# Norm weights turned by TensorE, the first two transfers mixed by chunks, the last left half in two pieces, and a new table of due times

## The chip, the cores and the metric

The kernel runs on one core of one Trainium2 chip. The metric is the device time of one execution, in microseconds (us). The kernel before takes 917.24 us, the median of three runs (917.19 to 917.48).

A core has TensorE (PE in the profile; its weight loads are PEld), VectorE (DVE), ScalarE (ACT), GpSimd (POOL) and SyncE (SP). Each works through its own list in order and waits on counts (semaphores) that the others raise. Transfers are issued by SP, ACT or POOL and carried out by 16 shared DMA engines.

## The reference, cut to what matters

One layer of a decoder trunk on x (512 positions x 1024) and a memory of 256 rows x 1024, all float32.

```python
h = rmsnorm(x, norm_mix_g);  proj = h @ w_in            # 9216 columns
y_a = (gb * conv3(gc * v)) @ w_a_out                    # short gated convolution
y_b = silu(layernorm(conv31(u * sigmoid(ug)))) @ w_b_out
memn = rmsnorm(mem, norm_mem_g);  k, vm = split(memn @ w_kv)
y_c = softmax(q k^T / 16) vm @ w_att_out                # 4 heads
x = x + (sum_i sigmoid(gate_i) * y_i) @ w_o
x = x + (silu(gt) * up) @ w_down                        # gt, up = split(conv3(rmsnorm(x) @ w_up))
return rmsnorm(x, norm_final_g)
```

## The kernel before, in words

Everything is on one core, with the features on the 128 partitions. A product is made of three matmuls: each operand is split into a rounded part (`whi`, `mh`, `zh`; a cast on ACT) and the rest (`wlo`, `ml`, `zl`; a subtraction on DVE), and hi x hi, lo x hi and hi x lo are added up in a PSUM bank (`product`). Weights come in units of 128 x 1024 (512 KB). SP fetches most of them; POOL adds sums of weight blocks by transfers of its own.

**The order of the work** is made when the program is built. PE's order is a list (`seq`), changed by MOVES. All other work is given as jobs, each with an engine, an estimated cost, what it needs and what it frees. `Jobs.run` then hands out the jobs: each job has a due time, counted back from the PE work that needs it, shifted by the table LATER, and AHEAD says how long before it the job may start. The result is one fixed list per engine.

**The start.** `jobs.first` lists the first transfers of SP: the first half of the memory (`mem`, turned by the host, 4 chunks of 128 features x 256 rows), then the first key unit of `w_kv` (`wf`), then value and key units. ACT issues one transfer of the norm weights (`pk`, 128 x 16: 8 columns of the memory's norm, 8 of the first norm of x). Meanwhile PE runs 11 products of a constant (L2101), which serve no result. ACT scales the 4 chunks by the norm weight (`mg0`, L950); then PE makes the first keys with 8 float32 products (L1142), 2 for each chunk, straight from `mg0` and the unit as it was fetched. After them come the values (L630 to L632), which need `mh`, `ml` (from `mg0`) and `whi`, `wlo` of the value unit in halves (L1087, L1091).

**The end of the up-projection.** The gated product `z` (L2069) is split into `zh`, `zl` and goes into the down-projection. In the same place DVE also splits weight units (`wlo`, L683) and combines PSUM banks (`uu`, L636), which gives a bank back to PE.

**The end.** Row tile 3 comes last. Its squares are summed, ACT takes the root (L2449), DVE the reciprocal (L2497). ACT scales the right half (L2455) and issues its store; DVE scales the left half with the norm weight (L2459, 128 x 512), and SP stores it.

## Time and profile before

| | |
|---|---|
| median of 3 runs | 917.24 us |
| profiled execution | 917.32 us |
| its span, first to last instruction | 915.5 us |
| PE busy | 906.7 us (99%) |
| DVE busy | 848.1 us (93%) |
| ACT busy | 685.3 us (75%) |
| PE's waits of over 0.15 us | 0.9, 1.0 and 0.5 us |
| DMA, mean over the span | 215 GB/s |

PE's matmuls overlap, and their ends are modelled: a PE that is busy all the time can still lose tenths of a microsecond between two matmuls. So the start of a matmul against the start of the one before is read as well. What lies ahead of PE's first product of use and behind its last one counts in full.

### The profile page before, as it was taken

The page shows a single profiled execution, that of the slowest core. Times are in us where ns is not written, and L with a number is a line of the kernel's source. Part 1 is how long each engine was busy: PE and PEld are TensorE (multiplying, and loading weights), DVE is VectorE, ACT ScalarE, POOL GpSimd, SP SyncE. Part 2 cuts the span into 40 slices and gives each one's busy share as a digit, 9 for nine tenths or more (in the row PEclk, how much of TensorE's full clock was granted, in tenths as well). Part 3 has the DMA queues.
Part 4 walks back from the last instruction along what each step waited for, and adds up shares of the span by engine and source line. Part 5 has one row for each costly group of instructions (what it writes and reads, how often), then busy time and mean ns, then how long its engine had stood idle before and what let it go on. Part 6 is the DMA issues. An engine that isn't in the chain of part 4 may idle for free.

```text
span 915.5 us, 17045 instructions
## 1 busy us (share of the span) xinstructions
PE 906.7 (99%) x6789; PEld 856.9 (94%) x6789; DVE 848.1 (93%) x965; ACT 685.3 (75%) x940; POOL 137.5 (15%) x164
## 2 busy tenths in 40 slices
PE   9999999999999999999999999999999999999997
PEld 8999999999989999999899997899999999988886
DVE  6996999999999998999898999898969899999987
ACT  7777979988987875979758973767757676865566
POOL 0111212000011111110101211121212021001400
PEclk9999999999999999999999999999999999999999
DMA  9998888644699878977868999999999677679972
GB/s 366 371 305 183 177 197 179 144 113 96 172 242 256 202 156 212 218 155 208 209 135 230 204 252 323 244 234 298 273 244 243 171 170 157 171 267 313 278 142 93
DMA packets 55377, 196.91 MB, mean 215 GB/s; under 512 B 6273, under 2 KB 6401, under 8 KB 55297
## 3 DMA queue, kind: packets, MB, share of 16 engines
q0 software_dynamic: 22608, 81.54, 49.3%
q1 hardware_dynamic: 32400, 114.02, 34.5%
q8 instruction: 53, 0.87, 0.4%
q10 hardware_dynamic: 288, 0.27, 0.1%
q14 instruction: 28, 0.22, 0.1%
HBM read 191.60 MB, written 4.19 MB: 214 GB/s over the span
## 4 chain that ended last, share of the span: by engine, by line
PE 95%; DVE 2%; ACT 1%; issue 1%; DMA 1%; SPq 0%; DVEq 0%; ACTq 0%
PE bank L862 63%; PE bank L632 6%; PE bank L630 6%; PE bank L631 6%; PE bank L1702 3%; PE bank L1700 3%; PE bank L1701 3%; PE bank L1153 2%; DVE wlo L683 1%; PE bank L1934 1%; DVE gtc L1656 1%; DMA wf<-in_w_kv 1%; PE bank L1142 0%; ACT whi L679 0%; PE bank L1989 0%
## 5 line engine op out<-in xcount | busy, mean ns | idle before, releaser
L679 ACT CAST whi<-wf 128x1024 fp32r<-128x1024 f32 (+1 forms) x199 | 207.1, 1044 | 88.8 <-PE bank L862 44.4
L683 DVE TENSOR_TENSOR wlo<-wf,whi 128x1024 fp32r<-128x1024 f32 (+1 forms) x193 | 232.1, 1211 | 16.1 <-ACT whi L679 15.8
L1468 ACT ACTIVATE tp<-u,pk 128x511 f32<-128x511 f32 (+22 forms) x184 | 119.0, 704 | 3.8 <-DVE acc L1475 3.2
L1475 DVE TENSOR_TENSOR acc<-acc,tp 128x1018 f32<-128x1018 f32 (+22 forms) x92 | 109.2, 1188 | 6.5 <-ACT tp L1468 4.7
L804 POOL DMA_DIRECT2D wf<-in_w_in x44 | 39.9, 937 | 204.4 <-DVE wlo L683 140.9
L862 PE MATMUL bank<-ft6h,whi 128*128 128x256 f32 x248 | 68.6, 277 | 0.5 <-ACT gt L889 0.5
L862 PE MATMUL bank<-fb10h,whi 128*128 128x256 f32 x248 | 68.7, 277 | 0.0
L862 PE MATMUL bank<-fb11h,whi 128*128 128x256 f32 x248 | 68.7, 277 | 0.0
L862 PE MATMUL bank<-ft7h,whi 128*128 128x256 f32 x248 | 68.6, 277 | 0.0
L862 PE MATMUL bank<-fb00l,whi 128*128 128x256 f32 x248 | 68.6, 276 | 0.0
L862 PE MATMUL bank<-ft7l,whi 128*128 128x256 f32 x248 | 68.5, 276 | 0.0
L862 PE MATMUL bank<-ft6l,whi 128*128 128x256 f32 x248 | 68.5, 276 | 0.0
L862 PE MATMUL bank<-ft5l,whi 128*128 128x256 f32 x248 | 68.5, 276 | 0.0
L862 PE MATMUL bank<-ft7h,wlo 128*128 128x256 f32 x248 | 68.5, 276 | 0.0
L862 PE MATMUL bank<-fb00h,whi 128*128 128x256 f32 x248 | 68.5, 276 | 0.0
L862 PE MATMUL bank<-ft5h,whi 128*128 128x256 f32 x248 | 68.5, 276 | 0.0
L862 PE MATMUL bank<-ft4h,whi 128*128 128x256 f32 x248 | 68.5, 276 | 0.0
L862 PE MATMUL bank<-ft6h,wlo 128*128 128x256 f32 x248 | 68.5, 276 | 0.0
L862 PE MATMUL bank<-ft4l,whi 128*128 128x256 f32 x248 | 68.5, 276 | 0.0
L862 PE MATMUL bank<-fb11l,whi 128*128 128x256 f32 x248 | 68.5, 276 | 0.0
L862 PE MATMUL bank<-fb10l,whi 128*128 128x256 f32 x248 | 68.5, 276 | 0.0
L862 PE MATMUL bank<-ft5h,wlo 128*128 128x256 f32 x248 | 68.5, 276 | 0.0
(414 smaller groups left out, 3165.3 us busy)
## 6 DMA issues: line engine op xcount, KB each, us to landing
wf<-in_w_in SPq DMA_DIRECT2D x52, 512.0 KB, 5.6
wf<-in_w_in POOLq DMA_DIRECT2D x44, 512.0 KB, 7.3
wf<-in_w_up SPq DMA_DIRECT2D x30, 512.0 KB, 7.8
wf<-in_w_up POOLq DMA_DIRECT2D x29, 512.0 KB, 8.1
wf<-in_w_down SPq DMA_DIRECT2D x15, 512.0 KB, 5.4
wf<-in_w_kv SPq DMA_DIRECT2D x8, 512.0 KB, 9.0
wf<-in_w_v SPq DMA_DIRECT2D x8, 512.0 KB, 7.9
wf<-in_w_att_out SPq DMA_DIRECT2D x8, 512.0 KB, 3.7
```

The lines of the kernel that those rows point to most:

```text
L630: nc.tensor.matmul(ps, s_hi, w_hi, start=start, stop=False, skip_group_check=again)
L631: nc.tensor.matmul(ps, s_hi, w_lo, start=False, stop=False, skip_group_check=again)
L632: nc.tensor.matmul(ps, s_lo, w_hi, start=False, stop=stop, skip_group_check=again)
L679: nc.scalar.copy(parts[0], src())
L683: nc.vector.tensor_tensor(lo, src(), hi.bitcast(F32), op=ALU.subtract)
L804: nc.gpsimd.dma_start(out=tiles[key], in_=block(w, col[c], k), accum_op=ALU.add)
L862: nc.tensor.matmul(to, w[:, k, at], col, start=first and n == 0, stop=k == 3 and n == 2, skip_group_check=again,)
L1468: nc.scalar.activation(two(("tp", p, s))[:, j, s:], two(("u", p))[:, j, : SEQ - s], AF.Copy, scale=weight(j),)
L1475: nc.vector.tensor_tensor(a, a, two(("tp", p, s))[:, :, s:], op=ALU.add)
L1700: nc.tensor.matmul(ps, w_hi[:, i, at], hi, start=first, stop=False)
L1701: nc.tensor.matmul(ps, w_hi[:, i, at], lo, start=False, stop=False)
L1702: nc.tensor.matmul(ps, w_lo[:, i, at], hi, start=False, stop=last)
```

## The change

**What is computed** stays the same. Five things are done in another way.

1. The host packs the first memory half and the first key unit into one array `first` of two parts: part e has chunks 2e and 2e+1 of both. SP fetches the two parts, 512 KB each, in place of the memory half and the unit.
2. The norm weights come as 16 rows of 128. PE turns them with a transposition between 6 and 4 products of the constant (10 in place of 11), and DVE copies the 16 columns out of the bank. `mg0` waits for that copy.
3. The 4 scaled chunks are made by ACT (0 and 2) and DVE (1 and 3) in place of ACT alone.
4. The last left half is scaled and stored in two pieces of 256 columns.
5. LATER, AHEAD, FRESH and MOVES have new entries throughout, so the lists of all engines are put in another order.

```diff
-    nc.scalar.dma_start(out=pk[:, :N_GAINS], in_=packed[:, :N_GAINS])
+    gain_rows = pk[:N_GAINS, N_GAINS : N_GAINS + P]
+    nc.scalar.dma_start(out=gain_rows, in_=gains)
...
+    for e in range(2):
+        job(("first tile", e), "NONE", 0.0, lambda e=e: make(("first", e)),
+            take=[(("first", e), ANY)])
+        job(("ldf", e), "SP", LOAD, lambda e=e: nc.sync.dma_start(
+            out=tiles["first", e], in_=first_in[e]), [("first tile", e)], LOAD_LATENCY,
+            use=[("first", e)])
...
-                for i in range(2 * e, 2 * e + 2):
-                    nc.scalar.activation(
-                        four(("mg0",))[:, i, :], four(("mem", 0))[:, i, :], AF.Copy,
-                        scale=par("norm_mem_g", i),
-                    )
+            def mem_scaled(i):
+                to, t = four(("mg0",))[:, i, :], first_part(i // 2, 0)[:, i % 2, :]
+                if i % 2:
+                    nc.vector.tensor_scalar(to, t, par("norm_mem_g", i), None, op0=ALU.mult)
+                else:
+                    nc.scalar.activation(to, t, AF.Copy, scale=par("norm_mem_g", i))
...
+                for i in (2 * e, 2 * e + 1):
+                    job(("mg0", i), "DVE" if i % 2 else "ACT", 0.36 if i % 2 else scaled_act(256),
+                        lambda i=i: mem_scaled(i), [("ldf", e), ("gains",), ("mg0 tile",)],
+                        use=[("first", e), source])
...
-    halved_unit(K0, block(w_kv, 0, 0), 4)
...
+    def warm_up(n, first=False):
+
+        ps = make(WARM) if first else tiles[WARM]
         some = mean_col.broadcast_to([P, P])
-        for i in range(11):
+        for i in range(n):
             nc.tensor.matmul(ps[:, :P], some, some, start=True, stop=True)
...
+    def gains_turned():
+        nc.tensor.transpose(tiles[WARM][:, P : P + N_GAINS], gain_rows, ident[:N_GAINS, :N_GAINS])
+
+    pe(("warm",), 2.6, lambda: warm_up(6, True), take=[(WARM, "ps")], unit=False)
+    pe(("turn",), 0.1, gains_turned, use=[WARM], unit=False)
+    pe(("warm", 1), 1.5, lambda: warm_up(4), use=[WARM], unit=False)
+    job(("gains",), "DVE", 0.1, lambda: nc.vector.tensor_copy(
+        pk[:, :N_GAINS], tiles[WARM][:, P : P + N_GAINS]), [("turn",)], use=[WARM])
...
-        job(("sl", t), "DVE", 0.67, lambda t=t: left_scaled(t), [("rc", t)])
+        for e, part in enumerate(ENDS if t == last else (slice(0, SEQ),)):
+            job(("sl", t, e), "DVE", 0.37 if t == last else 0.67,
+                lambda t=t, part=part: left_scaled(t, part), [("rc", t)])
+            job(("st", t, 0, e), "SP", STORE, lambda t=t, part=part: stored(t, 0, nc.sync, part),
+                [("sl", t, e)], LOAD_LATENCY)
...
-    "ACT cf": 470, "ACT exp": -1067.2, "ACT fh h b00": -451, "ACT fh h b10": -0.1,
+    "ACT c3": -709, "ACT cf": 1.1, "ACT csq": 2.7, "ACT exp": -1408.4, "ACT fh h b00": -55,
```

The first instructions of PE, before and after, with the counts that each waits for (`DMAHW..` are transfers, `bank` is a PSUM bank; in the kernel after, L2128 is the constant's product, L2131 the transposition, L1167 the first keys):

```order
L2101 MATMUL bank_100<-mean_col 128x128 [waits DVE_49]
L2101 MATMUL bank_100<-mean_col 128x128 x10
L1142 MATMUL bank_124<-mg_8_118,wf_96 128x256 [waits DMAHW2_49,Activation_49]
L1142 MATMUL bank_124<-mg_8_118,wf_96 128x256
L1142 MATMUL bank_124<-mg_8_118,wf_96 128x256 [waits Activation_49]
```

```order
L2128 MATMUL bank_100<-mean_col 128x128 [waits DVE_49]
L2128 MATMUL bank_100<-mean_col 128x128 x5
L2131 MATMUL bank_100<-ident,pk 128x16 [waits DMAHW1_49,Pool_49]
L2128 MATMUL bank_100<-mean_col 128x128 x4
L1167 MATMUL bank_122<-mg_6_107,first_95 128x256 [waits DMAHW0_49,Activation_49]
L1167 MATMUL bank_122<-mg_6_107,first_95 128x256
L1167 MATMUL bank_122<-mg_6_107,first_95 128x256 [waits DVE_49]
```

The transposition stands behind 6 products and ahead of 4. In the built program the 11 instructions from the first product of the constant to the last raise PE's count once, with the last of the 4.

The first instructions of DVE, before and after (`mg` is the scaled memory, `wlo` of `wf_97` the rest of the first value unit; L2136 is the copy of the turned weights):

```order
L622 MEMSET mean_col 128x1
L973 TENSOR_TENSOR ml_130<-mg_8_118,mh_129 128x512 [waits Activation_49] x2
L1091 TENSOR_TENSOR wlo_142<-wf_97,whi_141 128x512 [waits DMAHW3_49,Activation_49]
L1091 TENSOR_TENSOR wlo_142<-wf_97,whi_141 128x512 [waits Activation_49]
L683 TENSOR_TENSOR wlo_158<-wf_114,whi_157 128x1024 [waits DMAHW4_49,Activation_49]
```

```order
L631 MEMSET mean_col 128x1
L2136 COPY pk<-bank_100 128x16 [waits PE_49]
L970 TENSOR_SCALAR mg_6_107<-first_95,pk 128x256 [waits DMAHW0_49,DVE_49]
L992 TENSOR_TENSOR ml_128<-mg_6_107,mh_127 128x512 [waits Activation_49]
L970 TENSOR_SCALAR mg_6_107<-first_96,pk 128x256 [waits DMAHW2_49]
L992 TENSOR_TENSOR ml_128<-mg_6_107,mh_127 128x512 [waits Activation_49]
L1117 TENSOR_TENSOR wlo_143<-wf_97,whi_142 128x512 [waits DMAHW3_49,Activation_49]
L1117 TENSOR_TENSOR wlo_143<-wf_97,whi_142 128x512 [waits Activation_49]
```

Three instructions are new ahead of the first split of a value unit: the copy, which waits for PE, and the two scaled chunks.

DVE at the end of the up-projection, before and after (`z` is the gated product; `uu` is the combination that gives `bank_1167` back to PE):

```order
L683 TENSOR_TENSOR wlo_1195_9472<-wf_1157_9199,whi_1194_9471 128x1024
L1656 SCALAR_TENSOR_TENSOR upc_1183_9382<-uu_1166_9273,pk_87,upc_1183_9382 128x510
L683 TENSOR_TENSOR wlo_1191_9449<-wf_1169_9304,whi_1190_9448 128x1024
L2069 TENSOR_TENSOR z_7063<-upc_1183_9382,gtc_1188_9418 128x2x512
L636 SCALAR_TENSOR_TENSOR uu_1199_9508<-bank_1167_9276,uu_1199_9508 128x2x256
```

```order
L693 TENSOR_TENSOR wlo_1194_9473<-wf_1158_9203,whi_1193_9472 128x1024
L1681 SCALAR_TENSOR_TENSOR gtc_1190_9451<-gt_1149_9105,pk_87,gtc_1190_9451 128x510
L693 TENSOR_TENSOR wlo_1189_9447<-wf_1170_9307,whi_1188_9446 128x1024
L693 TENSOR_TENSOR wlo_1196_9503<-wf_1176_9344,whi_1195_9502 128x1024
L2094 TENSOR_TENSOR z_7065<-upc_1183_9384,gtc_1190_9451 128x2x512
L646 SCALAR_TENSOR_TENSOR uu_1178_9349<-bank_1167_9278,uu_1178_9349 128x2x256
```

One more split of a weight unit now stands between the split that PE takes next (`wlo_1191`, now `wlo_1189`) and the combination `uu`.

## Rows read from the trace of the kernel before

**Rows 1.** The page: span, and busy time of each engine
```profile
span 915.5 us, 17045 instructions
PE 906.7 (99%) x6789; PEld 856.9 (94%) x6789; DVE 848.1 (93%) x965; ACT 685.3 (75%) x940; POOL 137.5 (15%) x164
```
**Rows 2.** Timeline, first 10 us: start us, us, engine, line, operation
```profile
0.74 0.39 SPq L943 DMA_DIRECT2D mem<-in_mem_t  x1
0.77 0.39 ACTq L624 DMA_DIRECT2D pk<-in_packed  x1
...
0.93 4.19 PE L2101 MATMUL bank<-mean_col 128*128 128x128 f32 x22 [0.93 <-DVE mean_col L622]
...
4.97 1.71 ACT L950 ACTIVATE mg<-mem,pk 128x256 f32<-128x256 f32 x4 [2.64 <-DMA pk<-in_packed]
...
6.11 3.69 PE L1142 MATMUL bank<-mg,wf 128*128 128x256 f32 x16 [0.99 <-DMA wf<-in_w_kv]
...
9.45 0.58 PE L630 MATMUL bank<-whi,mh 128*128 128x512 f32 x1
...
9.87 0.39 PE L631 MATMUL bank<-wlo,mh 128*128 128x512 f32 x1
```
**Rows 3.** Waits of PE over the whole span: total us, times, longest
```profile
PE bank L862 <- ACT gt L889: 0.5, 1, 0.5
```
**Rows 4.** DMA landing of the tiles pk, mem and out, in that order
```profile
DMA to landing us min/median/max: 4.1/4.1/4.1
DMA to landing us min/median/max: 4.0/5.8/7.6
DMA to landing us min/median/max: 2.0/2.3/2.8
```
**Rows 5.** Busy time of L2101 by stretch: us, PE busy (records), PEld busy
```profile
0.93:4.06 3.13, 3.13 (x14) 3.13 (x15) 1.00 0.60 164
4.06:4.95 0.89, 0.89 (x10) 0.87 (x8) 1.00 1.00 398
```
**Rows 6.** Groups by line and form: count, busy us, mean ns of one, idle before
```profile
L2497 DVE RECIPROCAL cols<-cols 128x1 f32<-128x1 f32 x4 | 0.6, 160 | 1.4 <-ACT cols L2449 1.4
L1321 DVE TENSOR_SCALAR pr<-pr,cols 128x256 f32<-128x256 f32 x16 | 4.9, 351 | 0.3
L973 DVE TENSOR_TENSOR ml<-mg,mh 128x512 fp32r<-128x512 f32 x2 | 1.3, 690 | 6.3 <-ACT mh L962 6.3
L1091 DVE TENSOR_TENSOR wlo<-wf,whi 128x512 fp32r<-128x512 f32 x2 | 1.3, 684 | 0.0
L962 ACT CAST mh<-mg 128x512 fp32r<-128x512 f32 x2 | 1.1, 612 | 0.0
```
**Rows 7.** Timeline of DVE at the end of the up-projection
```profile
799.38 1.22 DVE L683 TENSOR_TENSOR wlo<-wf,whi 128x1024 fp32r<-128x1024 f32 x1
800.51 1.22 DVE L2069 TENSOR_TENSOR z<-upc,gtc 128x1024 f32<-128x1024 f32 x1
801.65 0.69 DVE L636 SCALAR_TENSOR_TENSOR uu<-bank,uu 128x512 f32<-128x512 f32 x1
```
**Rows 8.** Timeline of PE in the same place, and 20 us later
```profile
800.65 0.50 PE L631 MATMUL bank<-wlo,zh 128*128 128x512 f32 x1
...
803.32 0.28 PE L862 MATMUL bank<-ft4h,whi 128*128 128x256 f32 x1
...
823.14 0.50 PE L632 MATMUL bank<-whi,zl 128*128 128x512 f32 x1
```
**Rows 9.** Timeline: two adjacent DVE instructions of 256 columns, and the last 5 us
```profile
13.90 0.88 DVE L979 SCALAR_TENSOR_TENSOR ml<-mem,pk,mh 128x256 fp32r<-128x256 f32 x2
...
910.75 0.75 DVE L2459 SCALAR_TENSOR_TENSOR x<-x,cols,gfin 128x512 f32<-128x512 f32 x1
911.50 0.38 ACTq L2464 DMA_DIRECT2D out<-x  x1
911.53 0.33 SPq L2464 DMA_DIRECT2D out<-x  x1
```

More of the change, by code (lines that the diff above doesn't have):

```diff
@@ new lines @@
+    "ACT zh a": -1, "ACT zh c": -2.4, "ACT zh d": 285, "ACT zh e": 322, "ACT zh f": -52,
+    "ACT zh g": 15, "DVE CV": 6.6, "DVE c3": -2775, "DVE centre": -11.1, "DVE cf": 279,
[6 rows of a table added]
+    "DVE hd": -8, "DVE kl": -595.3, "DVE kt": 301, "DVE lns": 486.6, "DVE low": -121,
+    "DVE m scale": 719.2, "DVE mfold": 18, "DVE mfold2": -35, "DVE mgl a": -52.3, "DVE mgl b": 1.1,
+    "DVE mgl c": 185, "DVE mgl d": -230, "DVE mgl e": -63.4, "DVE mgl g": -3.1, "DVE ms c": -468,
+    "DVE ms d": 144.4, "DVE ms e": -42, "DVE ms f": -9, "DVE msum": -43, "DVE mu fold": -22,
@@ L149 @@
 }
 FRESH = {
[L152 to L153 removed]
+    (("glu", 2), 7), (("glu", 3), 3), (("cv", 1), 4), (("bb", 1), 1), (("bb", 1), 4),
+    (("mq", 0), 7), (("up", 0), 5), (("up", 0), 6), (("up", 0), 4), (("up", 2), 6),
 }
@@ new lines @@
+    ((("cv", 1), 3), (("bb", 0), 4)),
+    ((("bb", 0), 7), (("cv", 2), 2)),
+    ((("cv", 1), 4), (("bb", 0), 7)),
+    ((("cv", 1), 7), (("bb", 0), 2)),
+    ((("cv", 0), 3), (("bb", 0), 1)),
+    ((("cv", 1), 6), (("cv", 0), 3)),
+    ((("cv", 0), 4), (("cv", 1), 6)),
+    ((("cv", 1), 2), (("cv", 0), 4)),
+    ((("cv", 1), 1), (("cv", 1), 2)),
+    ((("cv", 0), 7), (("cv", 1), 1)),
+    ((("cv", 0), 6), (("bb", 0), 5)),
+    ((("cv", 0), 2), ("merge", 2, 1, 0)),
+    (("o", 3, 1), (("gate", 2, 1), 4)),
@@ L997, in mem_square @@
             make(("msq", g))
-            nc.scalar.activation(tiles["msq", g], tiles["mem", g], AF.Square)
-        job(("msq", g), "ACT", actv(1024), mem_square,
-            [("ldm", g, 0), ("wh", ("V", 0, 1))],
-            take=[(("msq", g), ANY)], use=[("mem", g)])
+            if g:
+                nc.scalar.activation(tiles["msq", g], tiles["mem", g], AF.Square)
+            else:
+                for e in range(2):
+                    nc.scalar.activation(
+                        two(("msq", g))[:, e, :], tiles["first", e][:, :512], AF.Square)
+        job(("msq", g), "ACT", actv(1024) if g else 2 * actv(512), mem_square,
+            ([("ldm", 1, 0)] if g else [("ldf", 0), ("ldf", 1)]) + [("wh", ("V", 0, 1))],
+            take=[(("msq", g), ANY)], use=[("mem", 1)] if g else [("first", e) for e in range(2)])
     def add_into(a, b):
@@ L1078, in halved_unit @@
             [("raw tile", s)], LOAD_LATENCY, use=[raw])
-        for e in range(2 if s == "V" else 0):
+        for e in range(2):
             at = slice(512 * e, 512 * (e + 1))
@@ L1138, in keys_product @@
         if (h, g) == (0, 0):
-            w, m = four(("raw", K0)), four(("mg0",))
+            w, m = first_part(ks[0] // 2, 1), four(("mg0",))
             for k in ks:
@@ L1191, in pe_keys @@
             for e in range(2):
-                pe(K0 if e else ("K0",), 4 * MM_WHOLE / 2,
-                   lambda e=e: keys_product(0, 0, (2 * e, 2 * e + 1)), [("ld0", "K"), ("mg0", e)],
-                   take=[] if e else [(bank, "ps")],
-                   use=[("raw", K0), ("mg0",)] + ([bank] if e else []), unit=False)
+                pe(("K", 0, 0) if e else ("K0",), 4 * MM_WHOLE / 2,
+                   lambda e=e: keys_product(0, 0, (2 * e, 2 * e + 1)),
+                   [("mg0", 2 * e), ("mg0", 2 * e + 1)], take=[] if e else [(bank, "ps")],
+                   use=[("first", e), ("mg0",)] + ([bank] if e else []), unit=False)
         else:
@@ L2123, in hybrid_block_kernel @@
         for side in sides
-    } | {("mg0", e) for e in range(2)}
+    } | {("mg0", i) for i in range(4)} | {("mg0 tile",), ("gains",)}
     GLU = [("glu", p) for p in range(4)]
@@ L2545 @@
     args["mem_t"] = a["mem"][0].T.reshape(2, 4, P, N_MEM).transpose(0, 2, 1, 3).reshape(2, P, 1024)
+    args["mem_t"], mem_0 = args["mem_t"][1], args["mem_t"][0]
+    args["first"] = np.concatenate(
+        [t.reshape(P, 2, 512).transpose(1, 0, 2) for t in (mem_0, units(a["w_kv"][0][:, :256])[0, 0])],
+        axis=2,
+    )
+    args["gains"] = np.concatenate([a[k].reshape(n, P) for k, n in PACKED[:2]], axis=0)
     args["packed"] = packed
```

188 lines of the change are left out of this document (84 added, 104 removed), and 162 rows, old and new, of tables (AHEAD, LATER).

## Prediction, written before the result

> **What bounds the kernel now.** I read the page first: the span is 915.5 us and PE is busy for 906.7 of it [rows 1]. So 8.8 us at most lie outside PE's work. Where they lie was read next, from the timeline's start and end and from the waits of PE. PE waits 0.93 us for its first instruction, and 0.99 us between the constant's products and the first keys [rows 2]; one wait in the middle is long enough to be listed, 0.5 us [rows 3]. The rest, some 6 us, is the tail behind the last matmul. The matmuls between are the same in both kernels. So the change can gain in three places: before the first keys, in short stalls of the middle, and in the tail. It can lose anywhere, since nearly every wait of PE is added to the time.
>
> The profiled execution took 917.32 us, 1.82 us more than its span; the sums below are made against it. It stands 0.08 us above the median of the runs.
>
> **The start, before.** The 16 records of the first keys begin at 6.11, 0.99 us late for the key unit [rows 2]. The scaled chunks began at 4.97, and what they waited for was not the memory (4.0 us from its issue at 0.74, so there at 4.74) but the norm weights: 4.1 us from 0.77, there at 4.88 [rows 2, 4]. The values begin at 9.45, and their second matmul at 9.87.
>
> **The start, after.** Both scaled chunks of the first part wait for the copy of the turned weights, and the copy waits for PE's count. That count is raised with the last of the 4 products behind the transposition. So the way is: weights landed, transposition, 4 products, copy, chunk, keys.
> - The constant's products are 22 records. Of the 10 that touch the last 0.89 us two reach in from before, so 8 begin there, 0.11 us each, the 2.4 GHz level, and 14 begin in the 3.13 us ahead, 0.22 each, the 1.2 GHz level [rows 5]. So the clock rose at about 4.06, and the first six products, 12 records, are through at about 4.06 - 2 x 0.21 = 3.64.
> - When 16 rows of weights land no row shows. The earliest is as the fastest store of 256 KB, 2.0 us after issue [rows 4]: 2.8. The latest is as the 128 rows of now: 4.88. I take the middle, 3.85, since the 128 pieces become 16, but pass the same queues beside the same 512 KB.
> - Transposition at 3.9, 0.1 us; 4 products are 8 records of 0.11 at the higher level: done at about 4.95. Their results are out some 0.16 us after the next could begin (a matmul's listed time against its step: 0.39 against 0.23 in [rows 2]): 5.1.
> - The copy of 16 columns: the nearest row is a small DVE instruction, 0.16 us [rows 6]. With 0.05 us for each count: 5.16 to 5.32.
> - The chunk on ACT: four take 1.71 us [rows 2], so one some 0.5 us to its end: 5.37 to 5.87. DVE's chunk takes 0.35 [rows 6] and is no later. Keys at 5.92 instead of 6.11: -0.2 us.
>
> Neither part of `first` is what ends this: the first lands at 4.74 like the memory before it (same size, same place in the queue), half a microsecond ahead of the copy, and the second where the key unit landed, ahead of the second half of the keys (5.92 + 1.67 = 7.6).
>
> Behind it: ACT casts `mh` only when DVE's chunk is there, and DVE does chunk 3 behind the first `ml`. With 0.61, 0.69 and 0.35 us [rows 6]: `mh` 6.5, `ml` 7.25, chunk 3 7.6, second `mh` 8.2, second `ml` 8.9, first `wlo` of the values 9.6 [0.68 in rows 6]. The second matmul of the values comes 0.42 us behind the first [rows 2], at 9.26 + 0.42 = 9.68. So this wait is covered, by 0.1 us; if the cover goes, it costs what is missing. In the kernel before, DVE had neither chunk nor copy ahead of it. Bounds of the start: weights at 2.8 leave the six products as the limit, turn at 3.7, keys at 5.7 (-0.4); weights at 4.88 give a turn at 4.93 and keys at 6.95 (+0.85).
>
> **The middle.** The new table moves instructions on all engines; PE's work is the same. Where the wait of 0.5 us stands (639 us), ACT's copy out of a bank stands behind a table load, a gate and two casts in both lists; I leave the wait in. At the end of the up-projection DVE sets the pace: PE's L631 at 800.65 starts 0.05 us behind the split that ended at 799.38 + 1.22 = 800.60, and DVE has no gap from there [rows 7, 8]. Now one more split stands ahead of `z` and `uu`. A split costs 800.51 - 799.38 = 1.13 us, so `uu` ends at 801.65 + 0.69 + 1.13 = 803.47; PE needs the bank at 803.32 [rows 8] and waits some 0.2 us. That split is then no longer due behind `uu`, so DVE is not later in sum, and the wait for `zl` that delays the matmul at 823.14 shrinks by as much (that matmul and the one at 800.65 are listed 0.50 us long, one that did not wait 0.39 [rows 2, 8]). Sum for the middle: 0. Its bounds are a second listed wait of the same kind not covered, 1.1 us or two splits' time (+2.2) on the one side, and on the other the listed wait and those two gone (-0.5 - 2 x 0.1 = -0.7).
>
> **The end.** DVE's left half takes 0.75 us from 910.75; both stores are issued at 911.50 and 911.53 [rows 9] and land up to 2.8 us later, the slowest of all stores [rows 4], while a store on its own takes 2.0. So the two are in each other's way. Two instructions of 256 columns take 0.88 us, the first about 0.48 [rows 9]: the first piece is issued at 911.26, 0.27 us earlier, the second at 911.66, 0.13 later. The right half is untouched and was last. With a quarter of the bytes ahead of the others, of the 0.8 us that the two cost each other a third should go: -0.25. Bounds: +0.13 (the last issue decides) and -0.8 (no more conflict).
>
> The Trainium skill, "DMA: Bandwidth & Descriptors", section on the anatomy of one DMA, says a transfer has a fixed cost of about 2.0 us, most of it the receipt of the last byte. By that the smaller last piece saves nothing, its later issue counts, and the end would be +0.13 instead of -0.25; the weights, on the other hand, could land at 2.8. The trace agrees in part: 2.0 us for the fastest store of 256 KB, but 2.8 for the same size beside another.
>
> **The sum.** -0.2 + 0 - 0.25 = -0.45 against 917.32: 916.9; less the 0.08 by which that execution stood above the median: 916.8 us.
>
> **The rivals.**
> - *The clock stays low (slower).* The clock rose at 4.06 after PE had worked without a pause since 0.93 [rows 2, 5]. Now PE pauses from 3.64 to 3.9, before that rise. If the rise is put off by it, the 4 products take 8 x 0.21 = 1.7 us instead of 0.9 (keys at 6.75, +0.65), and the 16 records of the keys, 3.34 us now, up to twice that: +0.65 + 3.34 - 0.25 gives 921.0 at the worst, 919.3 if it rises after half of the keys. It decides from the moment that the pause is long enough to matter, which no row tells; for it speaks that the pause is new, against it that it is short beside 2.7 us of work. By the Trainium skill, "TensorE: Matmul & The Clock Gate", part 1, activity releases a clock that is throttled by default; that a pause can delay it follows, and no run here shows it.
> - *The weights come as early as a transfer can.* Keys at 5.7 and the stores out of each other's way: -0.4 - 0.5: 916.3.
> - *The keys start behind the first part*, as if the copy were done by then: chunk from 4.8, keys at 5.35 (-0.76), with the waits of the middle gone (-0.7) and the end -0.25: 915.5, and below it where the stores gain more. Against it stands the count that the last product raises.
> - *The table leaves a new wait.* One split too late where DVE has no gap, not given back: +1.1 to +2.2, less 0.45: 917.9 to 919.0, and more for each further split.
> - *Late weights*: as now, +0.85 - 0.25: 917.8.
>
> **How the numbers follow.** My forecast has 0.55, early weights 0.15, the keys behind the first part 0.06, the table's wait 0.12, late weights 0.06, the low clock 0.06. Within 0.2% of before is 915.4 to 919.1 us, about what a measurement can tell from no change. Forecast, early and late weights lie in it, most of the table's wait too; below it most of the case behind the first part, where the stores gain more than I take; above it the low clock and a third of the table's wait, with more than two splits late. That makes faster 0.05, same 0.85, slower 0.10. The range leaves the low clock and the far ends of the others out: 915.7 to 918.4.
>
> **What would show it.** Right: the transposition at about 3.9 and the keys at 5.8 to 6.0, with ACT's chunk waiting for DVE's copy rather than a transfer; the constant's last 4 products at 0.11 us a record; `wlo` of the values just ahead of PE; a short wait of PE for `uu` near 803; the last stores' landing at most 2.6 us. Wrong: keys before 5.5 or behind 6.5, records of the keys at 0.43, or a listed wait of PE in the middle that is longer than 0.5 us.

## The result, and the profile after

The changed kernel takes 918.54 us, the median of 22 executions (917.48 to 921.53). The kernel before, run beside it, takes 917.60 (22 executions, 917.19 to 918.69). The ratio is 1.0014, with an interval from 1.0007 to 1.0020: 0.1% slower, where 916.8 was predicted with a range up to 918.4. Slower is not all: the executions of the changed kernel also spread over 4 us, those of before, beside them, over 1.5.

The profiled execution took 918.20 us. The page:

```profile
span 916.4 us, 17058 instructions
PE 908.0 (99%) x6788; PEld 857.6 (94%) x6788; DVE 849.7 (93%) x969; ACT 684.2 (75%) x939; POOL 137.1 (15%) x164
```

The span is 0.9 us longer than before [rows 1]. Three stretches make it up, each read from the start of one instruction to the start of another.

**The start: 0.80 us later.** Timeline of the kernel after (start us, us, engine, line, operation):

```profile
3.80 0.27 PE L2131 MATMUL bank<-ident,pk 16*128 16x16 f32 x1
4.00 2.08 PE L2128 MATMUL bank<-mean_col 128*128 128x128 f32 x8
6.11 0.17 DVE L2136 COPY pk<-bank 128x16 f32<-128x16 f32 x1 [5.24 <-PE bank L2128]
6.32 0.51 ACT L972 ACTIVATE mg<-first,pk 128x256 f32<-128x256 f32 x1 [3.99 <-DVE pk L2136]
6.88 3.72 PE L1167 MATMUL bank<-mg,first 128*128 128x256 f32 x16 [0.81 <-ACT mg L972]
10.25 0.58 PE L640 MATMUL bank<-whi,mh 128*128 128x512 f32 x1
```

The norm weights were not late, and the chunk waited for DVE's copy, not for a transfer. Landing of the tiles `pk` and `first`, in that order:

```profile
DMA to landing us min/median/max: 2.9/2.9/2.9
DMA to landing us min/median/max: 3.7/4.1/4.5
```

Late is what stands between transposition and copy. Stretches of the constant's products (from:to, length, PE busy with the number of records):

```profile
0.93:3.65 2.72, 2.72 (x12) 2.63 (x12) 1.00 0.64 184
4.00:5.87 1.87, 1.87 (x8) 1.78 (x8) 1.00 1.01 407
```

Behind the transposition 8 records take 1.87 us. That is 0.213 us a record and 0.16 more for the first, the same rate as ahead of it: the 1.2 GHz level throughout, where before the clock had risen at 4.06 [rows 5]. (The column of the granted clock, the 1.00 behind PEld, reads 1.00 here in both kernels, before the first recorded change of the clock; so the level is read from what a record takes.) The copy then waits for the last of these products and starts at 6.11, where the prediction had 5.16; the keys start at 6.88, before at 6.11 [rows 2]. Their records run at the higher level: 16 of them from 6.88 to 10.25, as before from 6.11 to 9.45. So the clock rose between 5.87 and 6.88.

**The middle: 0.4 us longer.** From the first value to the last matmul PE needs 910.13 - 10.25 = 899.88 us; before it was 908.91 - 9.45 = 899.46. The last matmul, after and before, and PE's two listed waits of the middle after:

```profile
910.13 0.28 PE L642 MATMUL bank<-whi,zl 128*128 128x256 f32 x1
```

```profile
908.91 0.28 PE L632 MATMUL bank<-whi,zl 128*128 128x256 f32 x1
```

```profile
PE bank L872 <- ACT gt L899: 0.5, 1, 0.5
PE bank L872 <- DVE uu L646: 0.2, 1, 0.2
```

The wait of 0.5 stayed [rows 3]. The one for `uu` is new. At the end of the up-projection, DVE and PE:

```profile
800.61 2.35 DVE L693 TENSOR_TENSOR wlo<-wf,whi 128x1024 fp32r<-128x1024 f32 x2
802.88 1.22 DVE L2094 TENSOR_TENSOR z<-upc,gtc 128x1024 f32<-128x1024 f32 x1
804.01 0.68 DVE L646 SCALAR_TENSOR_TENSOR uu<-bank,uu 128x512 f32<-128x512 f32 x1
...
804.85 0.36 PE L872 MATMUL bank<-ft4h,whi 128*128 128x256 f32 x1 [0.17 <-DVE uu L646]
```

Two splits stand ahead of `z`, and PE waits 0.17 us. The long matmul at 823.14 [rows 8] has no successor: none of this kind lasts over 0.41 us there now. Another part of the 0.4 us lies in the run of 48 key matmuls between the first values and the sums of the squares (`ss`). Its first matmul and the first one behind it, after and then before:

```profile
15.94 0.28 PE L1178 MATMUL bank<-mh,whi 128*128 128x256 f32 x1
...
21.59 0.50 PE L1043 MATMUL ss<-mean_col,msq 128*128 128x1 f32 x4
```

```profile
15.13 0.28 PE L1153 MATMUL bank<-mh,whi 128*128 128x256 f32 x1
...
20.60 0.50 PE L1017 MATMUL ss<-mean_col,msq 128*128 128x1 f32 x4
```

The run takes 5.65 us after and 5.47 before, 0.2 more: the matmuls follow each other every 0.118 us in place of 0.114. What slows them no row tells. Not every execution of the changed kernel has it: the run takes 5.47 in e9 and e14, 5.65 in e13. In the five profiles with the start of before (before, e5, e7, e8, e12) it takes 5.46 to 5.47, so whether the new start makes it likelier is open.

**The end: 0.3 us shorter.** From the last matmul to the end of the span 916.4 - 910.13 = 6.3 us, before 915.5 - 908.91 = 6.6. The last three stores (KB each, us to landing), in the order of their issue at 912.48, 912.72 and 912.90:

```profile
out<-x SPq DMA_DIRECT2D x1, 128.0 KB, 1.8
out<-x ACTq DMA_DIRECT2D x1, 256.0 KB, 2.2
out<-x SPq DMA_DIRECT2D x1, 128.0 KB, 2.4
```

Before, ACT's last store took 2.8 us [rows 4] and landed last, beside one of the same size. Now it takes 2.2 and is no longer last. The second piece is: from the start of the last matmul it lands after 912.90 + 2.4 - 910.13 = 5.2 us, where ACT's store landed after 911.50 + 2.8 - 908.91 = 5.4.

The prediction weighed a rule of the Trainium skill ("DMA: Bandwidth & Descriptors", anatomy of one DMA): a fixed cost of about 2.0 us, by which a smaller piece saves nothing. The section gives its figures for transfers issued by GpSimd, and it has a second part, bytes over 436 GB/s, which the prediction left out; from that, an estimate, 128 KB should land 0.3 us sooner than 256. The trace shows nearly that difference: the first piece takes 1.8 us, the fastest store of 256 KB 2.0 [rows 4]. Beside another store both sizes take longer, 2.4 and 2.8.

### The profile page after: what moved, and what is told of

Same layout as the page of the kernel before. It is cut to its first block, busy times and chain, and to the rows that moved or that the text cites. A ratio compares the mean times of both kernels' runs of the same rounds, so it can differ in the third digit from the quotient of the medians.

```text
span 916.4 us, 17058 instructions
## 1 busy us (share of the span) xinstructions
PE 908.0 (99%) x6788; PEld 857.6 (94%) x6788; DVE 849.7 (93%) x969; ACT 684.2 (75%) x939; POOL 137.1 (15%) x164
## 4 chain that ended last, share of the span: by engine, by line
PE 96%; DVE 3%; ACT 1%; issue 0%; DVEq 0%; ACTq 0%
PE bank L872 62%; PE bank L640 6%; PE bank L641 6%; PE bank L642 6%; PE bank L1726 3%; PE bank L1727 3%; PE bank L1725 3%; PE bank L1178 2%; DVE wlo L693 1%; PE bank L1959 1%; DVE gtc L1681 1%; PE bank L2128 1%; PE bank L1167 0%; PE bank L2014 0%; PE bank L1421 0%
## 5 line engine op out<-in xcount | busy, mean ns | idle before, releaser
L689 ACT CAST whi<-wf 128x1024 fp32r<-128x1024 f32 (+1 forms) x203 | 211.4, 1046 | 98.1 <-PE bank L872 55.1
L693 DVE TENSOR_TENSOR wlo<-wf,whi 128x1024 fp32r<-128x1024 f32 (+1 forms) x197 | 237.1, 1211 | 11.9 <-ACT whi L689 11.3
L872 PE MATMUL bank<-ft4h,wlo 128*128 128x256 f32 x248 | 68.5, 276 | 0.0
L872 PE MATMUL bank<-fb00h,wlo 128*128 128x256 f32 x248 | 68.5, 276 | 0.0
```

The lines of the kernel that those rows point to most:

```text
L689: nc.scalar.copy(parts[0], src())
L693: nc.vector.tensor_tensor(lo, src(), hi.bitcast(F32), op=ALU.subtract)
L872: nc.tensor.matmul(to, w[:, k, at], col, start=first and n == 0, stop=k == 3 and n == 2, skip_group_check=again,)
```

## The experiments

Every kernel was timed beside the kernel before, on the same chip; e1 to e4, e5 to e8, e9 and e10, e11 and e12, and e13 to e16 are such groups. The weights land 2.7 to 3.7 us after issue: 2.7 to 3.0 in e1 to e3, e6 and e11, 3.3 to 3.7 in e9, e10 and e13 to e16, on other chips, and on one chip from 3.3 to 3.7 (e13 to e16). So kernels of two groups are compared by what each stands over the kernel before of its own group. "Low records" is how many of the keys' 16 took 0.43 instead of 0.216 us in the profiled execution.

| | products ahead, behind | keys at | low records | values at | median (lowest to highest) us | over before | over 919.5 |
|---|---|---|---|---|---|---|---|
| before, with e1 to e4 | 11, no turn | 6.11* | 0 | 9.45* | 917.37 (917.00 to 919.81) | | 1 of 27 |
| after, first runs | 6, 4 | 6.88 | 0 | 10.25 | 918.54 (917.48 to 921.53) | 0.94 | 7 of 22 |
| e1 | 10, 0 | 6.58 | 8 | 11.80 | 918.20 (917.12 to 920.11) | 0.83 | 3 of 11 |
| e2 | 3, 4 | 6.97 | 6 | 11.75 | 920.48 (919.90 to 921.35) | 3.11 | 5 of 5 |
| e3 | 6, 0 | 5.11 | 9 | 10.48 | 918.31 (916.21 to 919.47) | 0.94 | 0 of 11 |
| e4 | 11, no turn | 5.34 | 0 | 8.71 | 917.41 (916.63 to 918.40) | 0.04 | 0 of 11 |
| e5 | 6, no turn | 5.88 | 6 | 10.70 | 919.23 (917.01 to 920.47) | 1.91 | 4 of 11 |
| e6 | 6, 3 own bank | 5.52 | 0 | 8.89 | 917.02 (916.38 to 919.78) | -0.30 | 1 of 11 |
| e7 | 11, no turn | 6.07 | 0 | 9.41 | 917.02 (916.74 to 920.15) | -0.30 | 1 of 11 |
| e8 | 11, no turn | 6.11 | 0 | 9.45 | 917.54 (917.36 to 920.72) | 0.22 | 1 of 11 |
| e9, after again | 6, 4 | 6.43 | 0 | 9.80 | 918.99 (917.57 to 921.57) | 1.85 | 5 of 10 |
| e10, old table | 6, 3 own bank | 6.20 | 10 | 11.57 | 924.92 (922.71 to 926.52) | 7.78 | 6 of 6 |
| e11 | 8, 3 own bank | 6.30 | 0 | 9.63 | 917.20 (916.55 to 920.28) | -0.26 | 1 of 11 |
| e12 | 14, no turn | 6.90 | 0 | 10.17 | 917.10 (916.83 to 919.48) | -0.36 | 0 of 11 |
| e13, after again | 6, 4 | 7.63 | 13 | 13.84 | 922.17, one run | | |
| e14, after again | 6, 4 | 7.29 | 6 | 12.15 | 920.26, one run | | |
| e15 | 6, 4 | 7.30 | 6 | 12.05 | 923.06, one run | | |
| e16 | 6, 4 own bank | 5.76 | 0 | 9.13 | 918.73 (917.38 to 920.83) | 1.51 | 2 of 10 |

\* its profile from the first part of this document. Medians of before in the other groups: 917.60 (first runs), 917.32 (e5 to e8; highest 920.95, 2 of 33 over 919.5), 917.14 (e9, e10), 917.46 (e11, e12), 917.22 (e13 to e16).

**e1: all products ahead.**

```diff
-    pe(("warm",), 2.6, lambda: warm_up(6, True), take=[(WARM, "ps")], unit=False)
+    pe(("warm",), 4.1, lambda: warm_up(10, True), take=[(WARM, "ps")], unit=False)
...
-    pe(("warm", 1), 1.5, lambda: warm_up(4), use=[WARM], unit=False)
```

> All 10 products of the constant stand ahead of the transposition, none behind; everything else is as in the changed kernel. Theory A (the pause of PE ahead of the transposition puts off the rise of the clock, and DVE's copy waits for the four products behind it): PE works without a pause from 0.93 us, the records go from 0.21 to 0.11 us near 4.06 as in the kernel before, the products end near 4.7, the transposition starts near 4.75, the first keys at 5.6 to 5.8 (before 6.11, changed 6.88). The time is about 1.1 us below the changed kernel, 0.2 to 0.4 below the kernel before, and single runs spread as narrowly as those of before. Rival B (the clock rises late for a reason that has nothing to do with the pause, and only the order of the count matters): all records at 0.21, products through at 5.2, keys at 6.2, about 0.7 us below the changed kernel, and the spread stays wide. Rival C (the loss is the new table's, in the middle): keys earlier, but the time stays at the changed kernel's.

Measured: ratio 1.0009 (1.0000 to 1.0018). No theory as it stood. Timeline:

```profile
0.93 4.63 PE L2128 MATMUL bank<-mean_col 128*128 128x128 f32 x20 [0.93 <-DVE mean_col L631]
...
6.58 5.57 PE L1167 MATMUL bank<-mg,first 128*128 128x256 f32 x16 [0.81 <-ACT mg L972]
```

20 records in 4.63 us are all at the low level, though PE did not pause. And the keys, listed 5.57 us long in place of 3.72, began low: PE idled 0.81 us ahead of them, while copy and chunk were made. So even without a pause the rise need not come by 4.06, nor by 5.35, where the step of the last of the 20 ends (0.93 + 0.16 + 20 x 0.213); and the keys can run low though PE had no pause ahead of the transposition. One execution of the 11 took 917.12; seven stand from 918.02 to 918.26, three at 920.

**e2: a longer pause; e3: none behind.** First the edit of e2, then that of e3.

```diff
-    pe(("warm",), 2.6, lambda: warm_up(6, True), take=[(WARM, "ps")], unit=False)
+    pe(("warm",), 1.3, lambda: warm_up(3, True), take=[(WARM, "ps")], unit=False)
```

```diff
-    pe(("warm", 1), 1.5, lambda: warm_up(4), use=[WARM], unit=False)
```

> 3 products of the constant stand ahead of the transposition in place of 6; the 4 behind it stay, so PE pauses from about 2.2 to 3.8 us and the copy is made at the same time as in the changed kernel at the low level. Theory A: the longer pause puts the rise of the clock off further, past 6.03 us, so some or all of the 16 records of the first keys take 0.43 us in place of 0.216: the second matmul group (values) comes 1 to 3.4 us later than at 10.25, and the time is 1 to 3.4 us above the changed kernel. Rival B (the rise does not hang on the pause): keys at 6.9, records at 0.216, the time of the changed kernel within 0.3 us.

> 6 products ahead of the transposition and none behind it, so that DVE's copy waits for the transposition alone. Theory A: transposition at 3.8, copy at 4.0 to 4.2, first chunk when the first part is there (4.43), keys start near 5.1, but PE has done less by then and pauses for 1.1 us more, so the clock is still low: some or all records of the keys take 0.43 us, and the values start at 9.5 to 11.8. Time between 0.8 below and 1.5 above the changed kernel, with a wide spread. Rival B (the clock is not tied to what PE does at the start): keys at 5.1 with records at 0.216, values near 9.3 or earlier, 1 us or more below the changed kernel.

Measured: e2 1.0032 (1.0020 to 1.0045), e3 1.0008 (1.0000 to 1.0017). The keys of e2 and of e3:

```profile
6.97 5.13 PE L1167 MATMUL bank<-mg,first 128*128 128x256 f32 x16 [0.81 <-ACT mg L972]
```

```profile
4.12 0.17 DVE L2135 COPY pk<-bank 128x16 f32<-128x16 f32 x1 [3.24 <-PE bank L2131]
...
5.11 5.72 PE L1167 MATMUL bank<-mg,first 128*128 128x256 f32 x16 [1.04 <-ACT mg L972]
```

e2 goes as theory A has it. Ahead of the copy it differs from the changed kernel by three products less, and so by a pause of 1.5 us in place of 0.15; what the missing work does by itself and what the pause does is not told apart. All five executions are at 919.9 or above. In e3 the copy is 0.3 us behind the transposition and the keys start 1.8 us earlier than in the changed kernel. But 9 of their records are low, and the values come 0.2 later than there. What an early start gains the low level takes back.

**e4: weights as before.** The transfer of 128 x 16, 11 products, no transposition and no copy; the rest as changed.

```diff
-    gain_rows = pk[:N_GAINS, N_GAINS : N_GAINS + P]
-    nc.scalar.dma_start(out=gain_rows, in_=gains)
+    nc.scalar.dma_start(out=pk[:, :N_GAINS], in_=packed[:, :N_GAINS])
...
```

> The norm weights come as before (128 x 16, one transfer, no transposition, no copy, 11 products of the constant without a pause); mixed transfers, chunks on two engines, the split store and the new table stay. Theory A: the clock rises near 4.06, weights land near 4.88 as before, chunks made by two engines side by side from 4.95, keys at 5.45 to 5.6 (before 6.11, changed 6.88). The time is 1.2 to 1.4 us below the changed kernel and 0.4 to 0.6 below the kernel before, with a narrow spread. Rival C (the loss is the table's, in the middle): keys as early, but no more than 0.4 us below the changed kernel. Rival D (the mixed transfers themselves land later): keys at 6.0 or later.

Measured: 0.9998 (0.9989 to 1.0007), 0.04 us over before where the changed kernel stands 0.94 over it. Keys at 5.34, a little earlier than expected; nothing over 918.40. Of the expected gain on before, 0.4 to 0.6, nothing is left: the values start 0.74 earlier than before, but from there PE needs 900.55 us to its last matmul, 1.1 more than before. Of that, 0.5 goes by 42 us (e6 shows such a place), and 0.5 between 590 and 610 us, where the matmuls follow each other more slowly without a listed wait; e13 loses as much there, the first profile of the changed kernel nothing.

**e5: the pause alone, in the kernel before.**

```diff
-        for i in range(11):
+        for i in range(6):
```

> The kernel before with 6 products of the constant in place of 11, and nothing else changed, so that PE pauses from about 3.65 us to the first keys at 6.11. Theory A, as the first four runs leave it (the rise of the clock comes at a moment that differs from one execution to the next, and only after PE has worked almost without a pause; any pause at the start puts it off, wherever it lies): the rise comes behind 8 us, half or more of the 16 records of the keys take 0.43 us, the values come 1.7 to 3.4 us later than at 9.45, and the median is 1.5 to 3.4 us above the kernel before. Rival B (the rise is late in some executions whatever PE does; the changed kernel only meets it more often since its keys start late): the median stays within 0.3 us of the kernel before, with single runs up to 2 us above.

Measured: 1.0019 (1.0010 to 1.0028). Theory A by the median and by the late rise; the profile, of an execution below the median (918.57), has fewer low records (6) and later values by less (1.25) than it named.

```profile
5.88 5.18 PE L1142 MATMUL bank<-mg,wf 128*128 128x256 f32 x16 [2.02 <-DMA wf<-in_w_kv]
```

Five products that compute nothing are worth 1.9 us of median: without them the keys, on time, run low. This rules out rival B, a rise that comes late whatever PE does: its median would have stayed within 0.3 us of before.

**e6: the copy freed from the products.** `warm_up(6)` as in the changed kernel, and behind the transposition:

```diff
-    pe(("warm", 1), 1.5, lambda: warm_up(4), use=[WARM], unit=False)
+    FILL = ("bank", "fill")
+    pe(("warm", 1), 1.0, lambda: warm_up(3, FILL), take=[(FILL, "ps")], unit=False)
...
```

> The changed kernel with 3 products behind the transposition in place of 4, and these write a bank of their own, so that DVE's copy waits for the transposition alone and PE works while copy and chunk are made. Theory A: transposition at 3.8, copy near 4.1, chunk near 4.55, products through by 5.45 at the latest, keys at 5.3 to 5.5; as PE now pauses for less than 0.5 us in all, the rise comes by 7 us in nearly every execution and at most half of the keys' records take 0.43 us. Median 0.9 to 1.3 us below the changed kernel (as it stands to before: 0 to 0.4 us below before), no run 2 us above the fastest. Rival B: keys as early, but the spread of e1 and e3 stays (3 us) and the median is at most 0.5 us below the changed kernel.

Measured: 0.9996 (0.9987 to 1.0005), by the medians 0.30 us below before, nine of eleven executions from 916.38 to 917.12. Theory A, but for one execution at 919.78, 3.4 above the fastest.

```profile
4.08 1.65 PE L2128 MATMUL bank<-mean_col 128*128 128x128 f32 x6
4.19 0.17 DVE L2137 COPY pk<-bank 128x16 f32<-128x16 f32 x1 [3.32 <-PE bank L2131]
...
25.79 0.68 DVE L1522 TENSOR_TENSOR xsq<-xsq 128x512 f32<-128x512 f32 x1
...
26.62 1.02 PE L1043 MATMUL ss<-mean_col,xsq 128*128 128x1 f32 x8
```

The copy is made right behind the transposition, and the keys start at 5.52. The lead of 0.56 us at the values does not last. At 26.62 PE needs the sums of x's squares, which DVE makes from 25.79; before it made them from 25.73, and PE came at 26.77. The next values start at 27.50 against 27.57. So in this execution no more than 0.15 us of what the start gains could pass this place; the rest of e6's gain is its tail. (In e4 the lead is still 0.53 there and 0.23 at 42 us.)

**e7: the split store alone. e8: the new table alone.** Into the kernel before, e7 takes the lines of the change on the left half (point 4), e8 the four tables (point 5).

```diff
-        job(("sl", t), "DVE", 0.67, lambda t=t: left_scaled(t), [("rc", t)])
+        for e, part in enumerate(ENDS if t == last else (slice(0, SEQ),)):
...
```

> The kernel before with the last left half scaled and stored in two pieces, nothing else. If the two pieces are what shortens the tail (6.64 us from the start of the last matmul to the end of the span before, 6.30 in the changed kernel and in all four runs so far): tail 6.3, time 0.3 us below before. Rival (the tail is shorter because the new table issues the earlier stores differently): tail 6.6, no difference.

> The kernel before with the new LATER, AHEAD, FRESH and MOVES, start and end as before. From the start of the first keys to the start of the last matmul PE needs 902.80 us before and 903.25 in the changed kernel. Theory (that 0.45 us is the table's): 903.1 to 903.4 here and the time 0.3 to 0.5 us above before, with a wait for uu of 0.2 near 804. Rival (it is owed to the start, which hands the stretch up to 45 us another rhythm): 902.7 to 902.9, time within 0.15 us of before.

Measured: e7 1.0000 (0.9991 to 1.0009), median 0.30 below before; tail 6.29 us. The split is worth 0.3 us by the tail, though the times alone can't show it. e8 1.0003 (0.9994 to 1.0011), median 0.22 above; from first keys to last matmul 909.04 - 6.11 = 902.93, 0.13 more than before. So the table costs 0.1 us and not 0.45, with the wait of 0.2 for `uu` as forecast. Its tail is 6.79, 0.15 longer than before.

**e9: the changed kernel again. e10: e6 with the table of before.**

> The changed kernel as it is, once more, for the spread of its executions and for a second profile. Theory A (the moment of the clock's rise differs from one execution to the next, and the pauses at the start put it off in most): single runs from 917.5 to 921.5, median 0.8 to 1.4 us above the kernel before; in the profile the records of the constant's last four products take 0.213 us, and the later the rise, the more of the keys' 16 records take 0.43, with the values later than 10.25 by 0.21 for each of them. Rival (the first profile was typical and the spread comes from elsewhere, the middle or the tail): rise near 6.0 again, values near 10.25, whatever the time of the run.

> The kernel of e6 (3 products behind the transposition in a bank of their own) with the LATER, AHEAD, FRESH and MOVES of before. If the new table is what eats the earlier start at 26 us (in e6 PE waits there for the last sum of the squares of x, and a lead of 0.56 us at 8.89 is 0.07 at 27.50): values near 8.9, the lead at 27.5 at least 0.3 us, time 0.2 to 0.4 us below e6, 0.5 to 0.8 below before. Rival (what PE waits for there comes with the transfers of x, whatever the table): lead at 27.5 below 0.15 us, time within 0.2 us of e6. As these due times were set for another start, a new wait of 0.2 us or more elsewhere is possible under either.

Measured: e9 1.0024 (1.0013 to 1.0036): five executions from 917.57 to 918.04, five from 919.93 to 921.57. Its profile is of an early one (917.64): the weights land at 4.2, the four products run high, the keys start at 6.43 (theory A had named the low level for the four, the rival values near 10.25 instead of 9.80: both missed). e10 1.0082 (1.0070 to 1.0094): 7.8 us above before. It can't answer its question, because its own keys began low and its middle, 906.74 us from the first value to the last matmul, is 7.3 longer than before and has new waits:

```profile
PE bank L865 <- DVE wlo L686: 2.2, 2, 1.3
PE bank L865 <- DVE ft5l L775: 1.7, 1, 1.7
```

So the old due times do not fit the new start as they are.

**e11: 8 products ahead, in e6. e12: 14 products, in e7.**

```diff
-    pe(("warm",), 2.6, lambda: warm_up(6), take=[(WARM, "ps")], unit=False)
+    pe(("warm",), 2.6, lambda: warm_up(8), take=[(WARM, "ps")], unit=False)
```

```diff
-        for i in range(11):
+        for i in range(14):
```

> The kernel of e6 with 8 products of the constant ahead of the transposition in place of 6 (3 behind it, in a bank of their own, and the new table, as there). In e9 and e10 the weights landed at 4.2 and 4.5 us instead of 3.7, so PE paused up to 1.1 us behind 6 products; 8 of them last until 4.5 at 0.213 us a record. Theory A: hardly a pause ahead of the transposition in any execution, keys at 5.5 to 5.9, the rise by 7 us in nearly every execution; median 916.9 to 917.2, 0.1 to 0.4 us below before, and fewer single runs over 918 than e6 has (2 of 11) or before has. Rival B (the rise hangs on nothing that PE does): runs over 918 as often as in e6, and e9's half of all.

> The kernel of e7 (before, with the split store) with 14 products of the constant in place of 11, so that PE works without a pause until 7.0 us if the clock stays low, and until 5.3 to 5.7 if it rises near 4 to 5. Theory A: where the rise comes early nothing changes, keys at 6.1; where it would have come late it now comes by 7.1 with the keys starting at 6.1 to 7.1, so runs more than 1 us above the fastest become rare (e7: 1 of 11; before: 8 of 33 over 918). Median 916.9 to 917.2, highest below 918.3. Rival B: median the same or up to 0.4 us later, and single runs over 919 as before.

Measured: e11 0.9995 (0.9986 to 1.0004), ten of eleven by 917.42; e12 0.9997 (0.9988 to 1.0006). Both medians fell as expected, 0.3 below before, which the intervals don't tell from no change. The late executions are too few in e7, e11 and e12 to count a difference, so theory A's second half isn't shown by them; e12's highest, 919.48, missed the 918.3 that it named. The profile of e11 is its one late execution (920.28), and it is another kind: the keys are all high, and a weight cast came late at 623 us.

```profile
PE bank L872 <- ACT whi L689: 1.0, 1, 1.0
```

From its first value to its last matmul PE needs 902.56 us, 3.1 more than before, and the wait is only 1.0 of it. Some 1.6 more goes between 650 and 690 us, where 341 matmuls are listed against 355 before; why is open.

In e12 the rise came late in an early execution. 28 records without a pause:

```profile
0.93:6.60 5.67, 5.67 (x26) 5.67 (x27) 1.00 0.82 293
6.60:6.90 0.30, 0.30 (x4) 0.27 (x2) 1.00 1.03 423
```

**e13 to e15: profiles of late executions; e16: the copy's wait alone.** e13 and e14 are the changed kernel. Of it, e15 has the last left half whole (first diff); e16 is e6 with 4 products behind (second), so all instructions and their order are the changed kernel's.

```diff
-        for e, part in enumerate(ENDS if t == last else (slice(0, SEQ),)):
+        for e, part in enumerate((slice(0, SEQ),)):
...
```

```diff
-    pe(("warm", 1), 1.0, lambda: warm_up(3, FILL), take=[(FILL, "ps")], unit=False)
+    pe(("warm", 1), 1.0, lambda: warm_up(4, FILL), take=[(FILL, "ps")], unit=False)
```

> The changed kernel as it is; a further profile, for what its late executions (over 919.5 us, 12 of the 32 timed so far) lose and where. Theory A: in a late one the rise of the clock lies behind 8 us, the records of the keys before it take 0.43 us, and the values start at 11.5 to 13.7 in place of 10.25; from the first value on PE needs 899.9 us to its last matmul, as in the first profile. Rival E (e11's profile: a weight cast that came 1.3 us late at 623 us, and nothing at the start): values at 9.8 to 10.3 and a wait of PE for a cast of 1 us or more in the stretch from 560 to 660 us. If this execution is an early one (below 918.5), it tells nothing of it.

> As e13: the changed kernel once more, since an execution is late in about one of three. Theory A: if late, values at 11.5 to 13.7; rival E: values by 10.3 and a wait of 1 us or more between 560 and 660 us.

> The changed kernel with the last left half scaled and stored whole, in one instruction and one transfer; the start is the same, so this profile too can show a late execution. The split: tail from the start of the last matmul to the end of the span 6.6 to 6.8 us (6.30 with the split in all profiles so far, 6.64 before, 6.79 in e8). Rival (the tail is the table's): 6.3. For the start: theory A and rival E as in e13.

> The changed kernel with its 6 and 4 products, where the 4 behind the transposition write a bank of their own; the number and order of all instructions are the changed kernel's, only what DVE's copy waits for is another. If the copy's wait for the four products is what makes the keys late: copy 0.2 to 0.4 us behind the start of the transposition, keys when the 4 products end: at 5.9 us at the low level (0.213 us a record), at 5.4 or earlier at the high one, in place of 6.88; PE's pause between products and keys is gone, runs over 919.5 become rare, median 917.0 to 917.4. Rival (the copy's wait costs little, the transposition does): keys at 6.5 or later, median over 918.

The profiles of e13, e14 and e15 are all late (922.17, 920.26, 923.06), and theory A holds for the place: values at 13.84 (0.14 later than its bound), 12.15 and 12.05. In e13 and e14 PE needs 900.26 and 900.04 us from there, nearly as in the first profile. e13:

```profile
4.56 0.26 PE L2131 MATMUL bank<-ident,pk 16*128 16x16 f32 x1 [0.70 <-DMA pk<-in_gains]
...
7.63 6.56 PE L1167 MATMUL bank<-mg,first 128*128 128x256 f32 x16 [0.81 <-ACT mg L972]
```

```profile
7.63:13.40 5.77, 5.77 (x14) 4.61 (x15) 1.00 1.03 420
```

PE waits at both ends of its four products, 13 of the 16 key records take 0.43 us, and that alone is 13 x 0.21 = 2.7 us. e15 has both: low keys, and a late cast of 0.6 us as in e11, with 902.54 us from the first value to the last matmul. Its tail is 6.67 without the split: the split again.

e16: 1.0018 (1.0008 to 1.0028). In its profile (917.38) the copy is freed and the keys start at 5.76:

```profile
4.50 0.20 PE L2131 MATMUL bank<-ident,pk 16*128 16x16 f32 x1 [0.64 <-DMA pk<-in_gains]
4.63 1.16 PE L2128 MATMUL bank<-mean_col 128*128 128x128 f32 x8
4.74 0.17 DVE L2137 COPY pk<-bank 128x16 f32<-128x16 f32 x1 [3.87 <-PE bank L2131]
...
5.76 3.72 PE L1167 MATMUL bank<-mg,first 128*128 128x256 f32 x16
```

But the median, 918.73, missed the expected 917.0 to 917.4, and two of ten are over 919.5. It stands 1.51 over before, the changed kernel 0.94 and 1.85 (e9): a gain by the copy's freeing alone can't be read from the times. On this chip the weights land at 4.4, so PE waits 0.64 us ahead of the transposition; freeing the copy cures the pause behind it, not this one. With 8 products ahead (e11) the median is 0.26 below before; but that is on another chip, where the weights landed earlier, so this last step is argued and not shown.

## Why the prediction was wrong

- **The step that failed: "4 products are 8 records of 0.11 at the higher level: done at about 4.95".** They took 0.21 each and the last began at 5.65, so copy, chunk and keys came 1 us later than forecast. That is most of the miss: -0.45 was forecast for the profiled pair and 0.9 measured. 0.11 rested on the rise at 4.06, read from one execution as if it were a property of the kernel. The runs show that it is not: where PE did not pause at all, the rise came at about 4.06 (before, e8), 4.6 (e4), 4.9 (e7) and 6.7 (e12), and in e1 not by 5.35; with pauses anywhere from 4.3 (e9, e16) to 13.4 (e13). The rise of the changed kernel's first profile, between 5.87 and 6.88, lies where kernels without a pause had it too. So that the pause of 0.15 us ahead of the transposition put it off in that execution is not shown; it may be the draw alone.
- **What the kernel before hid.** Its 11 products are 22 records, which end by 5.8 us even if all take 0.213 (0.93 + 0.16 + 22 x 0.213), and its keys wait until 6.1 for their unit. So a rise at any time up to 6 costs it nothing. The change put the products on the path to the keys, where the same variation becomes time, and opened two pauses. The keys run low in 8 of the 11 profiles of kernels that pause (e1, e2, e3, e5, e10, e13, e14, e15; not in the first profile, e9 and e16), and in none of the 7 others (before, e4, e7, e8, e12, and e6 and e11 with a pause of 0.25 and 0.14 us). e5 differs from before by nothing but the missing products. Over 919.5 are 14 of 34 executions of the changed kernel and 3 of 131 of before. How many of the 14 lost it at the start is not known: e11 and e15 lost 3.1 us in the middle, e15 besides its low keys.
- **The rival "the clock stays low" named it.** The priced parts were right: 1.7 us for the four products, keys at 6.75 (6.88), up to 921.0 (late executions reach 921.6, and 922.2 in e13). Not borne out were its chance of 0.06 and the ground given, a pause "short beside 2.7 us of work". The pause behind the products, 0.8 us while copy and chunk are made, was in the sum as a term of the path, and was not seen as a pause of PE.
- **Right:** the weights' landing (3.67 against 3.85), the transposition at 3.80, the chunk that waits for the copy, neither part of `first` on the path, `wlo` of the values in time, the wait of 0.5 that stays, the short wait for `uu` and the one at 823 that goes. The copy came 0.25 us behind the end of the last record's step (5.65 + 0.21), where 0.21 had been taken.
- **The end** was right in that the stores are less in each other's way (ACT's lands in 2.2 us for 2.8), and nearly in size: -0.3 for -0.25 (e7: 6.29, e15: 6.67). That the second piece would then be the last to land was not in it, and the third of 0.8 us that it took off was a choice, so the size is partly luck.
- **The middle** was set at 0. The table costs 0.1 (e8). Of the other 0.3 of the profiled pair, 0.2 is in the run of key matmuls, which is slow in some executions of the same kernel and not in others; why stays open.

The Trainium skill, "TensorE: Matmul & The Clock Gate", part 1, says that the point of the rise varies by 0.5 us either way from one run to the next, because what decides it does not start anew with the kernel. The runs agree that it moves, but by more: from 4.06 to 6.7 us without a pause. The prediction had taken from that page of the Trainium skill only that activity releases the clock.

A kernel that is surely faster than before was not found. e6, e7, e11 and e12 stand 0.3 to 0.4 us below it by their medians, which their intervals don't tell from no change; against the changed kernel, each taken over before of its own group, they gain 1.2 to 1.3 us.

## What to carry to other kernels

A moment in one profile at which the clock changes is one draw. Before putting work that serves no result on the path of work that does, price both levels for it, and look for what now waits for it: here a count raised by the last of several instructions in one bank, which another bank undoes. Ask of each gain at the start where PE next waits for something whose time does not move; in e6 that was at 26 us, and a lead of 0.56 us kept 0.07.

## What was not expected of the hardware

- The keys' float32 records take 0.43 us at the low level and 0.216 at the high one, and the level stayed low up to 13.4 us in e13, where PE waited for 0.70 and 0.81 us on the way.
- It can also fall again in the middle: in e10, behind waits of 0.65 and 0.86 us at 646 and 648 us, 16 matmuls of 256 columns took twice as long. Stretch by stretch, with the granted clock behind PEld:

```profile
648.70:652.10 3.40, 3.40 (x18) 3.40 (x18) 0.51 1.06 333
652.20:655.60 3.40, 3.40 (x32) 3.40 (x32) 1.00 1.06 243
```

- The same 8 KB of weights landed 2.7 to 3.7 us after their issue in different runs, and the first 512 KB beside them 3.5 to 4.4: what waits for these transfers has a spread of a microsecond.
- A store of 128 KB, issued 0.24 us ahead of the next, landed in 1.8 us, and one issued 0.18 us behind another in 2.4. Two of 256 KB, issued 0.03 us apart, took 2.6 and 2.8 before; the fastest of 256 KB took 2.0.
